# Rotated scores as two float32r products on stacked parts, and three steps moved in a hand-written order

## The chip, the cores and the metric

The kernel runs on one core of a Trainium2 chip. The metric is the device time of one execution in microseconds (us); the median over several runs is compared.

## The reference, cut to what matters

Two layers over `x` of 256 tokens by 1024 channels, all in float32. In each layer RMSNorm gives `h`, one combined projection of `h` feeds three branches, and each branch is multiplied by its own SiLU gate, projected back to 1024 channels, weighed by a sigmoid gate and summed. An output projection, another RMSNorm and the residual end the layer.

```python
# A: chunked gMLP.  sv is linear in the tokens; group g has its own 128 x 128 matrix
sv = einsum('gij,bnjgc->bnigc', ws_masked, layernorm(v)) + bs
a  = u * sv
# B: latent attention, 8 heads, 128 plain + 64 rotated channels, one rotated key for all heads
q = concat([q_nope, rope(q_rope)]);  k = concat([k_nope, rope(k_rope) for every head])
s = where(key_chunk <= query_chunk, q @ k.T / sqrt(192), -1e30)     # chunks of 64 tokens
b = softmax(s) @ v
# C: a causal convolution of width 4, then a gated linear recurrence over the tokens
xc = conv(x_c);  r, i = sigmoid(blocks(xc, w_a) + b_a), sigmoid(blocks(xc, w_x) + b_x)
```

The scores of one head are thus a product over 128 plain channels plus a product over 64 rotated ones.

## The kernel before, in words

**Precision.** A float32 product is slow on TensorE, and a float32r product is quicker but rounds its operands. Most products therefore work on operands in two parts: `hi` is the value rounded to float32r, `lo` the rest, and hi x hi + hi x lo + lo x hi is added up in PSUM (`mm3`; L307, L308, L309, or L431 to L433 where tokens are the rows of the result). The attention products are float32 products on whole values (L728 to L731, L770, L771).

**Weights.** They come in chunks, which are loaded, split and used in a fixed order: a DMA into a ring of three `raw` buffers, ScalarE's copy to `whi` (L268), VectorE's subtract to `wlo` (L269). There are three `whi`/`wlo` pairs. When a step has done with its chunk, it frees the pair, and the split of a later chunk is issued at that point on ScalarE and VectorE, behind what they already have in their queues. The table `LATE` says behind which stage of a step that is; for the query chunks (`uq`) it is stage 3, after the rotation, for `u` the end of its products.

**Order.** No scheduler orders the work. The table `ORDER` (L51 to L63) names the steps of a layer, and each step issues its instructions on all engines when its turn comes; every engine runs its own queue in that order. The steps that matter here:

- `uq` j: the queries of heads 2j and 2j + 1, rotated by VectorE (L645 to L647) into `qr`. Both heads share one tile: head 2j has partitions 0 to 63, head 2j + 1 partitions 64 to 127.
- `attend` i: the scores of heads 2i and 2i + 1 (i < 4), then `flip`, the transposes of the softmax of pair i - 1 (L759, six 128x128 blocks), then the `values` of pair i - 2 (L770, L771), then the softmax of pair i on VectorE and ScalarE (L737 to L752). So attend 4 has flip(3) and values(2), attend 5 has values(3).
- `split` g: the two parts `xh`, `xl` of the recurrence's input of group g: ScalarE's copy (L452) and VectorE's subtract (L453), of 128x1280 each.
- `norm` 0: the LayerNorm of `v` into `vn` (VectorE and GpSimd, L807 to L811). `stack` 0: copies of `xh` and `xl` into stacked tiles (VectorE's casts L449, ScalarE, GpSimd).
- `u` j, `za` j: two projections, then gMLP's gate. `za` j takes its projection into a bank, then the products with the gate matrix (L843, eight on 128 columns) into another one, `pm`; then ScalarE takes the sigmoid (L847) and VectorE multiplies (L848, L849) and reads `pm` (L852, twice).

**Rotated keys.** `krt[0]` has the rotated keys in partitions 0 to 63 and zeros in the others, `krt[1]` the other way round. The product of the shared `qr` tile with `krt[a]` so gives head 2i + a alone, at the price of half the rows being zero.

**PSUM.** There are two rings of banks: `bank`, five, for projections and scores, and `aux`, three (L133), for transposes, values, `pm` and others. A ring gives its banks out in turn, whoever asks; whoever gets one waits until its last user has been read.

Of the kernel before, what the change touches and what calls it, by code (L numbers as in the profile page):

```python
# [7 lines left out]
F32 = mybir.dt.float32  # L8
F32R = mybir.dt.float32r
AF = mybir.ActivationFunctionType  # L10
ALU = mybir.AluOpType
AX = mybir.AxisListType

P = 128
L = 2
D = 1024
S = 256
# [10 lines left out]
H, HN, HR, HV = 8, 128, 64, 128  # L28
# [23 lines left out]
    ("wl", 0), ("xc", 0), ("turn", 0), ("xc", 1), ("conv", 0), ("uq", 0), ("conv", 1), ("xc", 2), ("ukv", 0),  # L52
    ("conv", 2), ("ukv", 1), ("decay", 0), ("ws", 0), ("xc", 3), ("uq", 1), ("attend", 0), ("shift", 0),
    ("uq", 2), ("v", 0),
    ("attend", 1), ("xc", 4), ("conv", 3), ("v", 1), ("conv", 4), ("uq", 3), ("attend", 2), ("split", 1),
    ("v", 2), ("v", 3), ("attend", 3), ("split", 0), ("norm", 0), ("u", 0), ("stack", 0), ("attend", 4),
# [38 lines left out]
def tile_trunk(ctx: ExitStack, tc, I, out):  # L95
    nc = tc.nc
    const = ctx.enter_context(tc.tile_pool(name="const", bufs=1))
# [8 lines left out]
    def nm(s):  # L106
        n_[0] += 1
        return f"{s}_{n_[0]}"

    def slot(s, shape, dt=F32):  # L110
        n = 1
        for v in shape:
            n *= v
        t = sp.tile([P, SLOT_W], dt, tag="slot", name=nm(s))
        v = t[:, :n]
        if len(shape) == 2:
            v = v.rearrange("p (a b) -> p a b", b=shape[1])
        return v
# [23 lines left out]
    def f(x):  # L142
        return x.bitcast(F32)

    def v2(x, b):
        return x.rearrange("p (a b) -> p a b", b=b)

    mm = nc.tensor.matmul
    act = nc.scalar.activation
    V = nc.vector  # L150
    G = nc.gpsimd
# [16 lines left out]
    for l in range(L):  # L168
        for j in range(4):
            c0, n = ((C_CQ, QR), (C_CQ + QR, KVR + HR))[j // 2]  # L170
# [102 lines left out]
    def loads_to(i):  # L273
        while state["dma"] <= min(i, len(chunks) - 1):
            load(chunks[state["dma"]])
            state["dma"] += 1
# [16 lines left out]
    def get(*key):  # L293
        assert ids[key] < state["split"], key
        return chunks[ids[key]]

    def done(c, **how):
        pairs.append(c.pair)
        pump(**how)

    def fin(c, key, stage, **how):
        if LATE.get(key, 0) == stage:
            done(c, **how)


    def mm3(ps, lh, ll, rh, rl, start, stop):
        mm(ps, lh, rh, start=start, stop=False)  # L307
        mm(ps, lh, rl, start=False, stop=False)  # L308
        mm(ps, ll, rh, start=False, stop=stop)  # L309
# [6 lines left out]
    sinT = const.tile([P, S], F32, name="sinT")  # L316
    cosK = const.tile([P, NT, 64], F32, name="cosK")
    sinK = const.tile([P, NT, 64], F32, name="sinK")
    krt = [const.tile([P, S], F32, name=f"krt{i}") for i in range(2)]
    hT = [const.tile([P, NT, KT, P], F32R, name=f"hT{i}") for i in range(2)]  # L320
    X = const.tile([P, NT, D], F32, name="X")
    xm = const.tile([P, 2, S], F32R, name="xm")
# [133 lines left out]
    with tc.manual_schedule():  # L456
# [7 lines left out]
        load(chunks[0], parts=2, mid=lambda: nc.sync.dma_start(X[:, 1], I["x"][0, P : 2 * P, :]))  # L464
        state["dma"] = 1
        loads_to(2)
        for i in range(2):
            G.memset(krt[i], 0.0)
        nc.sync.dma_start(cosT, I["cosT"])
        nc.sync.dma_start(sinT, I["sinT"])  # L470
        nc.sync.dma_start(cosK, I["cosK"].rearrange("(t p) f -> p t f", p=P))
# [59 lines left out]
        for l in range(L):  # L531
# [53 lines left out]
            for i in range(8):  # L585
                j, t = (i // NT, i % NT) if l == 0 else (i % 4, i // 4)
# [7 lines left out]
            def turn_ranks(_):  # L594
                for b in range(3):
                    ps2 = aux()
                    for i in range(2):
                        k = 2 * b + i
                        for t in range(NT):
                            o = ps2[:, i * S + t * P : i * S + (t + 1) * P]  # L600
                            if k < 5:
                                nc.tensor.transpose(o, cn[t][:, k * P : (k + 1) * P], ident)
                            else:
                                nc.tensor.transpose(o[:64], krr[t], ident)
                    for i in range(2):
                        k = 2 * b + i
                        o = ps2[:, i * S : (i + 1) * S]
                        if k < 5:
                            act(cT[0][:, k], o, AF.Copy, scale=pt[:, k : k + 1])
                            V.scalar_tensor_tensor(  # L610
                                cT[1][:, k], o, pt[:, k : k + 1], f(cT[0][:, k]), ALU.mult, ALU.subtract
                            )
                        else:
                            act(krt[0][:64], o[:64], AF.Copy)
                            act(krt[1][64:], o[:64], AF.Copy)


            q = [slot("q", (4, S)) for _ in range(2)]
            kk = [slot("k", (4, S)) for _ in range(2)]
            vv = [slot("vv", (D,)) for _ in range(NT)]  # L620
            qr = slot("qr", (4, S))
            xp = [slot("xp", (GT, S + 3)) for _ in range(2)]
            xc = [slot("xc", (GT, S)) for _ in range(2)]
            for g in range(2):
# [2 lines left out]
            def queries(j):  # L627
                c = get(l, "uq", j)
                ps, ps2 = bank(), bank()
                for i in range(2):  # L630
                    for k in range(3):
                        a = i * P
                        mm3(ps[:, i * S : (i + 1) * S], c.h(k, a, a + P), c.l(k, a, a + P),
                            cT[0][:, k], cT[1][:, k], k == 0, k == 2)
                for k in range(3):
                    mm3(ps2[:, :S], c.h(k, S, S + P), c.l(k, S, S + P), cT[0][:, k], cT[1][:, k], k == 0, k == 2)
                fin(c, "uq", 0)
                act(q[j // 2][:, (j % 2) * 2 : (j % 2) * 2 + 2], v2(ps, S), AF.Copy)
                fin(c, "uq", 1)
                qs, qa = tmp(), tmp()  # L640
                for a in range(4):
                    b = a ^ 1
                    act(qs[a * 32 : a * 32 + 32, :S], ps2[b * 32 : b * 32 + 32, :S], AF.Copy)
                fin(c, "uq", 2)
                V.tensor_tensor(qa[:, :S], ps2[:, :S], cosT, ALU.mult)  # L645
                V.tensor_tensor(qs[:, :S], qs[:, :S], sinT, ALU.mult)
                V.tensor_tensor(qr[:, j], qa[:, :S], qs[:, :S], ALU.add)  # L647
                fin(c, "uq", 3)

            def keys_values(j):  # L650
                c = get(l, "ukv", j)
                for i in range(2):
                    ps = bank()
                    for m in range(2):
                        a = (2 * i + m) * 256
                        for k in range(2):
                            mm3(ps[:, m * S : (m + 1) * S], c.h(k, a, a + P), c.l(k, a, a + P),
                                cT[0][:, 3 + k], cT[1][:, 3 + k], k == 0, k == 1)
                    act(kk[j][:, 2 * i : 2 * i + 2], v2(ps, S), AF.Copy)
                for t in range(NT):  # L660
                    ps = bank()
                    ts = slice(t * P, (t + 1) * P)
                    for k in range(2):
                        rh = c.hi[:, k].rearrange("p (h r) -> p h r", r=256)[:, :, P:]
                        rl = c.lo[:, k].rearrange("p (h r) -> p h r", r=256)[:, :, P:]
                        lh, ll = cT[0][:, 3 + k, ts], cT[1][:, 3 + k, ts]
                        mm(v2(ps, P), lh, rh, start=k == 0, stop=False)
                        mm(v2(ps, P), lh, rl, start=False, stop=False)
                        mm(v2(ps, P), ll, rh, start=False, stop=k == 1)
                    if t == 1:  # L670
                        fin(c, "ukv", 0)
                    act(vv[t][:, j * 512 : (j + 1) * 512], ps, AF.Copy)
                fin(c, "ukv", 1)
# [48 lines left out]
            def scores(i):  # L722
                scs = [bank(), bank()]
                for a, sc in enumerate(scs):
                    h = 2 * i + a
                    qn, kn, kr = q[h // 4][:, h % 4], kk[h // 4][:, h % 4], krt[a]
                    qp = qr[:, i]
                    mm(sc[:, 0:P], qn[:, 0:P], kn[:, 0:P], start=True, stop=False)  # L728
                    mm(sc[:, 0:P], qp[:, 0:P], kr[:, 0:P], start=False, stop=True)
                    mm(sc[:, P : 3 * P], qn[:, P:], kn, start=True, stop=False)  # L730
                    mm(sc[:, P : 3 * P], qp[:, P:], kr, start=False, stop=True)  # L731
                return scs

            def softmax(scs):
# [324 lines left out]
            r = rsqrt_sum(ss)  # L1059
# [53 lines left out]
```

## Time and profile before

| | us |
|---|---|
| median of 3 runs | 798.22 (797.47 to 798.29) |
| the profiled execution | 798.34 |
| its span, first to last instruction | 796.6 |
| mean granted TensorE clock | 0.997 |
| TensorE products busy | 788.1 (99%) |
| VectorE / ScalarE / GpSimd busy | 548.9 (69%) / 469.3 (59%) / 70.5 (9%) |
| queue of the weight loads, share of 16 DMA engines | 54.3% |

In the timeline's rows stand: start in us, duration in us (of all instructions of the row), engine, source line, operation, result and operands, shapes, number of instructions, and in brackets how long the engine was idle before it and what ended that. Products overlap, so a PE row's duration is longer than its step to the next. A float32 product shows as two instructions, a float32r product as one. 1.74 us of the profiled execution lie outside its span.

### The profile page before, as it was taken

What the parts mean: (1) busy time and instruction counts of PE and PEld (TensorE: products, weight loads), DVE (VectorE), ACT (ScalarE), POOL (GpSimd) and SP (SyncE); (2) the same over time, 40 slices, a digit from 0 to 9 for tenths busy, and PEclk for the clock granted to TensorE, in tenths of its full rate; (3) what the DMA queues carried; (4) which work ended last, traced back from release to release, by engine and by line L of the source; (5) the groups of instructions that cost most, each with busy time, mean ns of one, the idle gap of its engine ahead of it and who ended that gap; (6) DMA issues with size and microseconds to landing.
All of it is one profiled execution on the core that took longest, in us unless ns stands there. A gap on an engine that the chain in (4) does not pass through costs nothing.

```text
span 796.6 us, 15355 instructions
## 1 busy us (share of the span) xinstructions
PE 788.1 (99%) x6445; PEld 780.2 (98%) x6445; DVE 548.9 (69%) x712; ACT 469.3 (59%) x689; POOL 70.5 (9%) x110
## 2 busy tenths in 40 slices
PE   9999999999999999999999999999999999999996
PEld 8999999999999999999999999999999999999996
DVE  5587788666876787555666868776578578775562
ACT  5785767339855736343567776654595584544441
POOL 1100503003000000000010032031210000000000
PEclk9999999999999999999999999999999999999998
DMA  7845454344666565666357626541575656564531
GB/s 229 290 152 182 153 161 155 112 122 137 201 213 211 159 215 169 199 212 216 109 171 239 208 94 211 159 128 51 166 219 167 221 162 202 185 214 150 193 132 54
DMA packets 134205, 137.87 MB, mean 173 GB/s; under 512 B 11046, under 2 KB 130808, under 8 KB 134136
## 3 DMA queue, kind: packets, MB, share of 16 engines
q1 hardware_dynamic: 134120, 136.90, 54.3%
q8 instruction: 50, 0.82, 0.4%
q14 instruction: 19, 0.16, 0.1%
q10 hardware_dynamic: 16, 0.00, 0.0%
HBM read 135.83 MB, written 1.05 MB: 172 GB/s over the span
## 4 chain that ended last, share of the span: by engine, by line
PE 94%; DMA 2%; issue 1%; DVE 1%; ACT 1%; SPq 0%; POOL 0%; POOLq 0%; DVEq 0%; ACTq 0%
PE mm L308 25%; PE mm L307 25%; PE mm L309 25%; PE mm L431 2%; PE mm L433 2%; PE mm L432 2%; DMA raw<-in_w_in_dram 1%; PE aux L843 1%; PE mm L730 1%; PE aux L770 1%; PE mm L731 1%; DMA X<-in_x_dram 1%; PE mm L549 1%; PE aux L1021 1%; PE mm L1020 1%
## 5 line engine op out<-in xcount | busy, mean ns | idle before, releaser
L269 DVE TENSOR_TENSOR wlo<-raw,whi 128x2048 fp32r<-128x2048 f32 (+5 forms) x123 | 264.6, 2156 | 115.9 <-ACT whi L268 115.5
L307 PE MATMUL mm<-hT,whi 128*128 128x256 f32 x1088 | 307.1, 282 | 0.0
L309 PE MATMUL mm<-hT,wlo 128*128 128x256 f32 x1088 | 305.8, 281 | 0.3 <-DVE wlo L269 0.3
L308 PE MATMUL mm<-hT,whi 128*128 128x256 f32 x1088 | 305.6, 281 | 0.0
L268 ACT ACTIVATE whi<-raw 128x2048 fp32r<-128x2048 f32 (+5 forms) x123 | 221.0, 1802 | 66.6 <-PE mm L308 26.8
L309 PEld LDWEIGHTS mm<-hT,wlo 128*128 128x128 f32 x1088 | 205.0, 188 | 0.5 <-DVE wlo L269 0.5
L307 PEld LDWEIGHTS mm<-hT,whi 128*128 128x128 f32 x1088 | 205.0, 188 | 0.0
L308 PEld LDWEIGHTS mm<-hT,whi 128*128 128x128 f32 x1088 | 205.0, 188 | 0.0
L973 ACT ACTIVATE t<-mm 128x512 f32<-128x512 f32 x18 | 10.8, 598 | 52.2 <-PE mm L309 52.2
L397 POOL TENSOR_TENSOR rstd<-rstd,mhalf 128x1 f32<-128x1 f32 x8 | 4.4, 551 | 391.1 <-DVE rstd L396 391.1
L308 PE MATMUL mm<-yc,whi 128*128 128x256 f32 x128 | 36.0, 282 | 0.0
L308 PE MATMUL mm<-ya,whi 128*128 128x256 f32 x128 | 36.0, 282 | 0.0
L307 PE MATMUL mm<-ya,whi 128*128 128x256 f32 x128 | 36.0, 281 | 0.0
L307 PE MATMUL mm<-yc,whi 128*128 128x256 f32 x128 | 36.0, 281 | 0.0
L431 PE MATMUL mm<-whi,hT 128*128 128x256 f32 x128 | 36.0, 281 | 0.0
L308 PE MATMUL mm<-yb,whi 128*128 128x256 f32 x128 | 35.9, 281 | 0.0
L309 PE MATMUL mm<-ya,wlo 128*128 128x256 f32 x128 | 35.9, 280 | 0.0
L309 PE MATMUL mm<-yc,wlo 128*128 128x256 f32 x128 | 35.9, 280 | 0.0
L309 PE MATMUL mm<-yb,wlo 128*128 128x256 f32 x128 | 35.8, 280 | 0.0
L307 PE MATMUL mm<-yb,whi 128*128 128x256 f32 x128 | 35.8, 280 | 0.0
L432 PE MATMUL mm<-wlo,hT 128*128 128x256 f32 x128 | 35.8, 279 | 0.0
L433 PE MATMUL mm<-whi,hT 128*128 128x256 f32 x128 | 35.7, 279 | 0.0
(279 smaller groups left out, 1663.4 us busy)
## 6 DMA issues: line engine op xcount, KB each, us to landing
raw<-in_w_in_dram SPq DMA_DIRECT2D x76, 1024.0 KB
raw<-in_w_proj_a_dram SPq DMA_DIRECT2D x8, 1024.0 KB
raw<-in_w_proj_b_dram SPq DMA_DIRECT2D x8, 1024.0 KB
raw<-in_w_proj_c_dram SPq DMA_DIRECT2D x8, 1024.0 KB
raw<-in_w_out_dram SPq DMA_DIRECT2D x8, 1024.0 KB
raw<-in_mla_w_uq_dram SPq DMA_DIRECT2D x8, 576.0 KB
raw<-in_mla_w_ukv_dram SPq DMA_DIRECT2D x4, 1024.0 KB
raw<-in_w_in_dram SPq DMA_DIRECT2D x4, 640.0 KB
```

The lines of the kernel that those rows point to most:

```text
L268: act(hi[:, w], c.raw[:, w], AF.Copy)
L269: V.tensor_tensor(lo[:, w], c.raw[:, w], f(hi[:, w]), ALU.subtract)
L307: mm(ps, lh, rh, start=start, stop=False)
L308: mm(ps, lh, rl, start=False, stop=False)
L309: mm(ps, ll, rh, start=False, stop=stop)
L431: mm(ps, lh, rh, start=k == 0, stop=False)
L432: mm(ps, lh, rl, start=False, stop=False)
L433: mm(ps, ll, rh, start=False, stop=k == KT - 1)
L549: mm(ps, ll, rh, start=False, stop=j % 2 * 4 + k == KT - 1)
L730: mm(sc[:, P : 3 * P], qn[:, P:], kn, start=True, stop=False)
L731: mm(sc[:, P : 3 * P], qp[:, P:], kr, start=False, stop=True)
L973: act(sg, ps, AF.Sigmoid)
```

## The change

**Scores.** `qr` now has a tile of its own per head, in float32r. The 64 rows of the head's own half hold the rounded part of its rotated query, the 64 rows of the other half the rest. `krt[0]` holds the rounded part of the rotated key in both halves, `krt[1]` the rest of it in both halves. The product of `qr` with `krt[0]` then adds hi x hi and lo x hi in one pass over 128 rows, the one with `krt[1]` hi x lo and lo x lo. Each head has two float32r products of 128 columns and two of 256 in place of one float32 product of each. The plain part stays float32. `krt` is no longer cleared by GpSimd. `queries` issues two copies (ScalarE) and two subtracts (VectorE) of 64x256 a chunk, after `fin(c, "uq", 3)`, so behind the split of the next weight chunk; the rotated keys get two subtracts a layer. The two tiles take one more of the 16 large slots.

**Order.** ("split", 1) moves from behind ("attend", 2) to behind ("u", 0). ("attend", 4) moves from before ("za", 0) to behind it.

```diff
--- before.py
+++ after.py
@@ -52,9 +52,9 @@
     ("wl", 0), ("xc", 0), ("turn", 0), ("xc", 1), ("conv", 0), ("uq", 0), ("conv", 1), ("xc", 2), ("ukv", 0),
     ("conv", 2), ("ukv", 1), ("decay", 0), ("ws", 0), ("xc", 3), ("uq", 1), ("attend", 0), ("shift", 0),
     ("uq", 2), ("v", 0),
-    ("attend", 1), ("xc", 4), ("conv", 3), ("v", 1), ("conv", 4), ("uq", 3), ("attend", 2), ("split", 1),
-    ("v", 2), ("v", 3), ("attend", 3), ("split", 0), ("norm", 0), ("u", 0), ("stack", 0), ("attend", 4),
-    ("za", 0), ("u", 1), ("za", 1), ("attend", 5), ("u", 2), ("za", 2), ("u", 3), ("za", 3), ("ga", 0),
+    ("attend", 1), ("xc", 4), ("conv", 3), ("v", 1), ("conv", 4), ("uq", 3), ("attend", 2),
+    ("v", 2), ("v", 3), ("attend", 3), ("split", 0), ("norm", 0), ("u", 0), ("split", 1), ("stack", 0), ("za", 0),
+    ("attend", 4), ("u", 1), ("za", 1), ("attend", 5), ("u", 2), ("za", 2), ("u", 3), ("za", 3), ("ga", 0),
     ("la", 0), ("lx", 0), ("r1", 0), ("stack", 1), ("pa", 0), ("ga", 1), ("pa", 1), ("la", 1), ("r2", 0),
     ("r3", 0), ("ga", 2), ("pa", 2), ("zb", 0), ("ga", 3), ("zb", 1), ("lx", 1), ("gb", 0), ("zb", 2),
     ("zb", 3), ("r1", 1), ("pa", 3), ("pb", 0), ("r2", 1), ("gb", 1), ("pb", 1), ("r3", 1), ("zc", 0),
@@ -316,7 +316,7 @@
     sinT = const.tile([P, S], F32, name="sinT")
     cosK = const.tile([P, NT, 64], F32, name="cosK")
     sinK = const.tile([P, NT, 64], F32, name="sinK")
-    krt = [const.tile([P, S], F32, name=f"krt{i}") for i in range(2)]
+    krt = [const.tile([P, S], F32R, name=f"krt{i}") for i in range(2)]
     hT = [const.tile([P, NT, KT, P], F32R, name=f"hT{i}") for i in range(2)]
     X = const.tile([P, NT, D], F32, name="X")
     xm = const.tile([P, 2, S], F32R, name="xm")
@@ -464,8 +464,6 @@
         load(chunks[0], parts=2, mid=lambda: nc.sync.dma_start(X[:, 1], I["x"][0, P : 2 * P, :]))
         state["dma"] = 1
         loads_to(2)
-        for i in range(2):
-            G.memset(krt[i], 0.0)
         nc.sync.dma_start(cosT, I["cosT"])
         nc.sync.dma_start(sinT, I["sinT"])
         nc.sync.dma_start(cosK, I["cosK"].rearrange("(t p) f -> p t f", p=P))
@@ -611,14 +609,16 @@
                                 cT[1][:, k], o, pt[:, k : k + 1], f(cT[0][:, k]), ALU.mult, ALU.subtract
                             )
                         else:
-                            act(krt[0][:64], o[:64], AF.Copy)
-                            act(krt[1][64:], o[:64], AF.Copy)
+
+                            for r in (slice(0, HR), slice(HR, P)):
+                                act(krt[0][r], o[:HR], AF.Copy)
+                                V.tensor_tensor(krt[1][r], o[:HR], f(krt[0][:HR]), ALU.subtract)
 
 
             q = [slot("q", (4, S)) for _ in range(2)]
             kk = [slot("k", (4, S)) for _ in range(2)]
             vv = [slot("vv", (D,)) for _ in range(NT)]
-            qr = slot("qr", (4, S))
+            qr = [slot("qr", (4, S), F32R) for _ in range(2)]
             xp = [slot("xp", (GT, S + 3)) for _ in range(2)]
             xc = [slot("xc", (GT, S)) for _ in range(2)]
             for g in range(2):
@@ -644,8 +644,15 @@
                 fin(c, "uq", 2)
                 V.tensor_tensor(qa[:, :S], ps2[:, :S], cosT, ALU.mult)
                 V.tensor_tensor(qs[:, :S], qs[:, :S], sinT, ALU.mult)
-                V.tensor_tensor(qr[:, j], qa[:, :S], qs[:, :S], ALU.add)
+                V.tensor_tensor(qa[:, :S], qa[:, :S], qs[:, :S], ALU.add)
                 fin(c, "uq", 3)
+
+
+                for a in range(2):
+                    own, other = (slice(i * HR, (i + 1) * HR) for i in (a, 1 - a))
+                    to = qr[j // 2][:, j % 2 * 2 + a]
+                    act(to[own], qa[own, :S], AF.Copy)
+                    V.tensor_tensor(to[other], qa[own, :S], f(to[own]), ALU.subtract)
 
             def keys_values(j):
                 c = get(l, "ukv", j)
@@ -723,12 +730,11 @@
                 scs = [bank(), bank()]
                 for a, sc in enumerate(scs):
                     h = 2 * i + a
-                    qn, kn, kr = q[h // 4][:, h % 4], kk[h // 4][:, h % 4], krt[a]
-                    qp = qr[:, i]
-                    mm(sc[:, 0:P], qn[:, 0:P], kn[:, 0:P], start=True, stop=False)
-                    mm(sc[:, 0:P], qp[:, 0:P], kr[:, 0:P], start=False, stop=True)
-                    mm(sc[:, P : 3 * P], qn[:, P:], kn, start=True, stop=False)
-                    mm(sc[:, P : 3 * P], qp[:, P:], kr, start=False, stop=True)
+                    qn, kn, qp = q[h // 4][:, h % 4], kk[h // 4][:, h % 4], qr[h // 4][:, h % 4]
+                    for o, ts, n in ((sc[:, 0:P], slice(0, P), P), (sc[:, P : 3 * P], slice(P, S), S)):
+                        mm(o, qn[:, ts], kn[:, :n], start=True, stop=False)
+                        mm(o, qp[:, ts], krt[0][:, :n], start=False, stop=False)
+                        mm(o, qp[:, ts], krt[1][:, :n], start=False, stop=True)
                 return scs
 
             def softmax(scs):
```

TensorE around attend 4 in the first layer, before (L759 transposes, L770 and L771 values; `aux_86` to `aux_88` are the three banks of the ring; the products of u 0 stand ahead of these rows, those of za 0 and then L843 into `aux_88` behind them):

```order
L759 MATMUL aux_88<-ident,t_75 128x128 [waits DVE_49,Activation_49]
L759 MATMUL aux_88<-ident,t_75 128x128 [waits DVE_49]
L759 MATMUL aux_88<-ident,t_75 128x128
L759 MATMUL aux_86<-ident,t_76 128x128 [waits DVE_49,Activation_49]
L759 MATMUL aux_86<-ident,t_76 128x128 [waits DVE_49]
L759 MATMUL aux_86<-ident,t_76 128x128
L770 MATMUL aux_87<-t_73,vv_387 128x256 [waits Activation_49]
L771 MATMUL aux_87<-t_73,vv_388 128x128
L770 MATMUL aux_87<-t_74,vv_387 128x256
L771 MATMUL aux_87<-t_74,vv_388 128x128
```

and with the change, where L849 is the gate product of za 0, L765 the transposes, L776 and L777 the values:

```order
L849 MATMUL aux_88<-wst_790,vn_979 128x128 [waits DVE_49,Activation_49]
L849 MATMUL aux_88<-wst_790,vn_980 128x128 [waits DVE_49]
L849 MATMUL aux_88<-wst_790,vn_979 128x128
L849 MATMUL aux_88<-wst_790,vn_980 128x128
L765 MATMUL aux_86<-ident,t_75 128x128 [waits Activation_49]
L765 MATMUL aux_86<-ident,t_75 128x128 x2
L765 MATMUL aux_87<-ident,t_76 128x128 [waits Activation_49]
L765 MATMUL aux_87<-ident,t_76 128x128 x2
L776 MATMUL aux_88<-t_73,vv_385 128x256 [waits DVE_49]
L777 MATMUL aux_88<-t_73,vv_386 128x128
L776 MATMUL aux_88<-t_74,vv_385 128x256
L777 MATMUL aux_88<-t_74,vv_386 128x128
```

The transposes and the values now stand behind za 0's gate products. The ring gives `aux_88` to the gate products, `aux_86` and `aux_87` to the transposes, and `aux_88` again to the values, which wait for a semaphore of VectorE (`DVE_49`) where they waited for one of ScalarE (`Activation_49`). In the second layer it is the same with `aux_87`.

VectorE in the same place, from the second tile of the LayerNorm to the reading of za 0's gate products, before:

```order
L811 TENSOR_SCALAR vn_963<-vn_963,st_32_399 128x1024
L269 TENSOR_TENSOR wlo_95<-raw_90,whi_94 128x2048
L449 CAST xs_1469<-xh_1406 64x512 x2
L449 CAST xm<-xl_1407 64x512 x2
L848 TENSOR_TENSOR t_79<-mm_81,t_79 128x512
L849 TENSOR_TENSOR t_79<-mm_85,t_79 128x512
L852 SCALAR_TENSOR_TENSOR t_80<-aux_88,pt_349,shift_404 128x256 x2
```

and with the change (L817, L854, L855 and L858 are the former L811, L848, L849 and L852):

```order
L817 TENSOR_SCALAR vn_980<-vn_980,st_33_398 128x1024
L269 TENSOR_TENSOR wlo_95<-raw_90,whi_94 128x2048
L453 TENSOR_TENSOR xl_1499<-xc_392,xh_1498 128x1280
L449 CAST xs_1502<-xh_1435 64x512 x2
L449 CAST xm<-xl_1436 64x512 x2
L854 TENSOR_TENSOR t_77<-mm_81,t_77 128x512
L855 TENSOR_TENSOR t_77<-mm_85,t_77 128x512
L858 SCALAR_TENSOR_TENSOR t_78<-aux_88,pt_347,shift_403 128x256 x2
```

The `xl` of split 1 has moved in between the weight split `wlo` and the casts of stack 0; before it stood some 30 rows earlier, behind the softmax of pair 2.

## The prediction

> **What bounds the kernel now.** I read the page's shares and the chain of waits first, then what TensorE (PE) waits for over the whole run.
>
> ```profile
> PE 788.1 (99%) x6445; PEld 780.2 (98%) x6445; DVE 548.9 (69%) x712; ACT 469.3 (59%) x689; POOL 70.5 (9%) x110
> PE 94%; DMA 2%; issue 1%; DVE 1%; ACT 1%; SPq 0%; POOL 0%; POOLq 0%; DVEq 0%; ACTq 0%
> ...
> PE aux L479 <- POOL ones L457: 1.0, 1, 1.0
> PE mm L549 <- DVE hT L505: 0.5, 1, 0.5
> PE mm L309 <- DVE wlo L269: 0.3, 1, 0.3
> ```
>
> The first row is busy time by engine, the second the chain that ended last by engine, the other three are all the waits of PE there are (us in total, times, longest). PE is busy in 788.1 of 796.6 us and waits 1.8 us in all. So two things pay in full: any time taken from a PE product, and any new wait of PE. VectorE (DVE) and ScalarE (ACT) have idle time, but only between the waits that tie them to PE.
>
> **The change: the products.** One head's scores before the change, on PE (start, us, instructions):
>
> ```profile
> 70.52 0.28 PE L307 MATMUL mm<-cT,whi 128*128 128x256 f32 x1
> 70.64 0.28 PE L308 MATMUL mm<-cT,whi 128*128 128x256 f32 x1
> 70.88 0.38 PE L728 MATMUL mm<-k,q 128*128 128x128 f32 x2
> 71.10 0.39 PE L729 MATMUL mm<-krt,qr 128*128 128x128 f32 x2
> 71.32 0.60 PE L730 MATMUL mm<-k,q 128*128 128x256 f32 x2
> 71.75 0.59 PE L731 MATMUL mm<-krt,qr 128*128 128x256 f32 x2
> 72.19 0.38 PE L728 MATMUL mm<-k,q 128*128 128x128 f32 x2
> ```
>
> Durations overlap, so the cost is the step from start to start. A float32 product is two instructions: L729 holds PE for 71.32 - 71.10 = 0.22 us, L731 for 72.19 - 71.75 = 0.44 us. A float32r product of 256 columns (L307, L308, operands in two parts) is one instruction with a step of 0.12 us. Two of them in place of L731 cost 0.24: a gain of 0.20 us a head. A float32r product of 128 columns is nowhere in this trace. If only the columns counted, it would step at half of 0.12, and two would cost 0.12 against 0.22 (a gain of 0.10). If it ran as slowly as the float32 product of its size, two would cost 0.44 (a loss of 0.22). The nearest row with one instruction on 128 columns and a fresh weight tile each is the transpose L759, shown below: six in 127.70 - 127.04 = 0.66 us, 0.11 each. I take 0.11, so that two cost what one float32 product did, and this half gains nothing. A head thus gains 0.20 (0.30 and -0.02 at the ends), a step of attention, two heads, 0.40 (0.60 and -0.04), and 16 heads 3.2 us (4.8 and -0.3).
>
> **The splits.** Each of eight query chunks adds two ACT copies and two DVE subtracts of 64x256, and each layer two DVE subtracts for the rotated keys. Nearest rows: 0.38 us a copy, 0.43 a DVE operation.
>
> ```profile
> L614 ACT ACTIVATE krt<-aux x2: 378/378/378, 41.9 to 431.6; 64x256 f32<-64x256 f32 x2
> ...
> 44.61 2.29 DVE L269 TENSOR_TENSOR wlo<-raw,whi 128x2048 fp32r<-128x2048 f32 x1 [2.77 <-ACT whi L268]
> 75.22 2.29 DVE L269 TENSOR_TENSOR wlo<-raw,whi 128x2048 fp32r<-128x2048 f32 x1 [0.72 <-ACT whi L268]
> 112.43 0.18 DVE L749 RECIPROCAL sum<-sum 128x4 f32<-128x4 f32 x1 [1.65 <-ACT t L747]
> ```
>
> That is 0.76 us of ACT and 0.86 of DVE a chunk. The brackets give DVE's idle time: behind the keys 2.77 us, behind the query chunks 0.72 and 1.65 us. PE hardly waits for DVE today, so I cost the splits at nothing. Without that cover they would be 0.9 us a chunk, 7 us in all. The two memsets that leave POOL save nothing, with POOL at 9%. No DMA is added or moved.
>
> **The moved steps.** Here the sum is decided. What PE does at the place in question, first layer:
>
> ```profile
> 127.04 0.82 PE L759 MATMUL aux<-ident,t 128*128 128x128 f32 x6
> 127.70 0.60 PE L770 MATMUL aux<-t,vv 128*128 128x256 f32 x2
> ...
> 128.93 0.36 PE L307 MATMUL mm<-hT,whi 128*128 128x256 f32 x1
> ...
> 134.69 1.05 PE L843 MATMUL aux<-wst,vn 128*128 128x128 f32 x8
> 135.50 0.36 PE L307 MATMUL mm<-hT,whi 128*128 128x256 f32 x1
> ```
>
> Six transposes (L759) and attention's values (L770, L771) take 128.93 - 127.04 = 1.89 us. Then comes za 0's projection, then its gate products L843, and at 135.50 projection u 1 starts. After the change the 1.89 us stand behind L843. All three kinds take banks of the `aux` ring, which has three: L843 one, the transposes two, and the values get the one that L843 has just filled. They must wait until DVE's L852 has read it. Before the change they took a bank that ACT had emptied long ago. DVE up to that L852:
>
> ```profile
> 126.70 1.49 DVE L453 TENSOR_TENSOR xl<-xc,xh 128x1280 fp32r<-128x1280 f32 x1
> ...
> 130.61 0.87 DVE L811 TENSOR_SCALAR vn<-vn,st 128x1024 f32<-128x1024 f32 x1 [0.45 <-POOL st L810]
> 131.40 2.48 DVE L269 TENSOR_TENSOR wlo<-raw,whi 128x2048 fp32r<-128x2048 f32 x1
> 133.80 1.16 DVE L449 CAST xs<-xh 64x512 fp32r<-64x512 f32 x2
> 134.98 1.06 DVE L449 CAST xm<-xl 64x512 fp32r<-64x512 f32 x2
> 136.06 0.69 DVE L848 TENSOR_TENSOR t<-mm,t 128x512 f32<-128x512 f32 x1
> 136.79 0.69 DVE L849 TENSOR_TENSOR t<-mm,t 128x512 f32<-128x512 f32 x1
> 137.40 0.86 DVE L852 SCALAR_TENSOR_TENSOR t<-aux,pt,shift 128x256 f32<-128x256 f32 x2
> ```
>
> From 131.40 on DVE has no gap: L852 ends at 138.26 because of the queue ahead of it. The second moved step puts one more `xl` (1.49 us, as at 126.70) into that queue, between `wlo` and the casts. What ties this stretch of DVE to PE lies earlier:
>
> ```profile
> 116.66 0.29 PE L433 MATMUL mm<-whi,hT 128*128 128x256 f32 x1
> 117.03 1.91 ACT L268 ACTIVATE whi<-raw 128x2048 fp32r<-128x2048 f32 x1 [1.12 <-issue]
> 118.98 2.29 DVE L269 TENSOR_TENSOR wlo<-raw,whi 128x2048 fp32r<-128x2048 f32 x1 [0.62 <-ACT whi L268]
> ```
>
> The last product of v 3 ends at 116.95, ACT's copy into the freed buffer starts at 117.03, DVE's subtract follows the copy. By then three of the layer's four steps of scores have run, so this anchor, and L852 with it, moves ahead by 3 x 0.40 = 1.20 us. L852 ends at 138.26 - 1.20 + 1.49 = 138.55. PE, four steps of scores ahead, has ended L843 at 135.50 - 1.60 - 1.89 = 132.01 and its six transposes at 132.67. It then **waits 5.9 us** for DVE. Queued behind the values are u 1 and everything after. The values take 128.93 - 127.70 = 1.23 us, and u 1 starts at 139.78 in place of 135.50: **4.28 us late**, the products' gain already taken off. The second layer is the same to a few hundredths:
>
> ```profile
> 524.76 0.36 PE L307 MATMUL mm<-hT,whi 128*128 128x256 f32 x1
> ...
> 526.65 0.87 DVE L852 SCALAR_TENSOR_TENSOR t<-aux,pt,shift 128x256 f32<-128x256 f32 x2
> ```
>
> 527.52 - 1.20 + 1.49 + 1.23 = 529.04 against 524.76, again 4.28. Together 8.6 us; at the ends of the products' gain (0.60 and -0.04 a step) the anchor moves by 1.80 or by -0.12, so 7.4 or 11.2 us. PE has no other idle time out of which the loss could be made up.
>
> **The clock.** A PE that stands still is throttled in this trace. At the start and the end of the run:
>
> ```profile
> 0.99 6.33 PE L479 MATMUL aux<-ones 128*128 128x128 f32 x28 [0.99 <-POOL ones L457]
> 7.26 0.22 PE L514 MATMUL aux<-ident,t 8*128 8x8 f32 x1
> ...
> 789.70 0.28 PE L1021 MATMUL aux<-whs,mg 128*128 128x256 f32 x1
> ...
> 790.00:792.00 2.00, 0.00 (x0) 0.00 (x0) 1.07 (x3) 0.47 (x2) 0.55 (x1) 1.00 0.00 0
> 792.00:794.00 2.00, 0.00 (x0) 0.00 (x0) 0.96 (x3) 0.00 (x0) 0.00 (x0) 0.56 0.49 176
> 794.00:797.00 3.00, 0.00 (x0) 0.00 (x0) 0.00 (x0) 0.00 (x0) 0.00 (x0) 0.50 0.18 60
> ```
>
> PE's last product ends at 789.98. In the three windows the granted clock (the last figure but two) is 1.00, 0.56 and 0.50: it halves at about 792.2, 2.3 us after PE stopped. A stall of 5.9 us is longer than that. At the start 28 instructions of L729's shape take 7.26 - 0.99 = 6.27 us, 0.224 each where the step is 0.11 at full speed: PE ran at half speed for 6.3 us of steady work, and lost 3.1. So a stall costs between nothing more (the clock holds) and 3.1 us more. I take 2.5, near the start's figure, a little below it because the start is a single case from a cold chip. Two stalls: 5.0 us.
>
> The Trainium skill's page "TensorE: Matmul & The Clock Gate" (Part 1: The HAM clock gate) says that the clock falls to half after an idle window of about 3.4 us, and comes back after one busy window of the same length. By its figure half speed would cost an estimated 1.7 us a stall and the sum would be some 1.6 us lower; the trace's 2.3 us to the fall and 6.3 us of slow start show that a single window isn't all that counts, so the rows are used.
>
> **The sum.** 798.34 (the profiled execution; the median of the runs, 798.22, lies 0.12 below) + 8.6 + 5.0 = 811.9, or **811.8 us** as a median.
>
> **The rivals.** (1) The stall comes, but the clock holds, or falls so late that little is lost. For it: only the end of the run shows the fall, and nothing there says that a stall between products counts alike. Against: 5.9 is well over 2.3 us. 798.3 + 8.6 = 806.9. (2) The float32r product of 128 columns is as slow as a float32 one, so nothing is gained: 798.3 + 11.2 + 5.0 = 814.5. For it: no row of such a product exists. Against: the transposes' 0.11. (3) The values find their bank free, PE doesn't stall, and the products' gain remains: 798.3 - 3.2 = 795.1, faster (793.5 with 4.8). The place is the second L852 of za 0, which would have to end by PE's 132.67 rather than 138.55; it decides from there on. Against: between 130.61 and L852's end DVE has 0.87 + 2.48 + 1.16 + 1.06 + 0.69 + 0.69 + 0.86 = 7.8 us of work without the moved `xl`, and `vn` itself waits for POOL. For it: only that DVE loses an `xl` some 13 us earlier, which the anchor at 117.03 doesn't pass on. (4) The stall is half as long, because DVE's queue runs 2.9 us further ahead than the anchor says: 798.3 + 8.6 - 5.8 = 801.1, and up to 804 with some loss of clock.
>
> **How the numbers follow.** Forecast 0.58, rival 1 0.20, rival 2 0.10, rival 3 0.07, rival 4 0.05. The time is the forecast's; its own range is 808.5 to 814. The range for 8 in 10 runs from rival 1 with the larger gain (798.2 + 7.4 = 805.6) to rival 2 with a little more (816). A measurement of this kernel can tell about 0.2%, 1.6 us, from no change: rivals 1, 2, 4 and the forecast all lie above it, rival 3 below. I leave 0.03 of rival 3 to the case in which a little is lost elsewhere and it ends within. Faster 0.06, same 0.03, slower 0.91.
>
> **What would show it.** Right, if PE's waits have a new row, the values' product on `aux` waiting for DVE's L858 (the changed file's number for L852), twice, near 5.9 us, and if the granted clock is under 1.00 in the windows right behind them. Steps of 0.12 for the two 256-column float32r products and 0.11 for the 128-column ones would confirm the gain; 0.06 or 0.22 its ends. The sum is wrong if that row is absent or under 2 us, if PE waits longer for `wlo` or a bank behind the query splits, or if za 0's L858 ends before PE's transposes do.

## The result

The changed kernel takes **819.56 us** (median) against 798.25 for the kernel before on the same chip, a ratio of 1.0255 (95% interval 1.0224 to 1.0286): slower. The prediction said slower, 811.8 us, with a range up to 816.0; the measured time lies 3.6 us above that range. One of the four executions took 1284.88 us at a mean granted clock of 0.557; the ratio leaves it out. The profiled execution took 819.68 us, its span is 817.7.

From the page of the changed kernel, busy time and the chain that ended last; then all that PE waits for (us in total, times, longest):

```profile
PE 792.7 (97%) x6445; PEld 784.4 (96%) x6445; DVE 558.1 (68%) x732; ACT 473.6 (58%) x705; POOL 71.4 (9%) x108
PE 90%; DVE 5%; issue 2%; ACT 1%; DMA 1%; POOL 1%; SPq 0%; POOLq 0%; DVEq 0%; ACTq 0%
...
PE aux L776 <- DVE t L858: 13.4, 2, 6.7
PE aux L849 <- DVE vn L817: 2.2, 4, 0.8
PE mm L545 <- ACT hT L501: 1.3, 1, 1.3
PE aux L477 <- POOL ones L457: 1.0, 1, 1.0
PE mm L547 <- DVE hT L503: 0.5, 1, 0.5
```

The first row of waits is the one forecast: the values' products wait for DVE to read za 0's gate products, once a layer. It is 6.7 us, not 5.9, and there is a second one ahead of it, L849 waiting for `vn`. PE is busy 4.6 us longer than before although its products got quicker, a sign of half speed. The place in the first layer, on PE, and the granted clock there (last figure but two of a window):

```profile
132.49 0.46 PE L849 MATMUL aux<-wst,vn 128*128 128x128 f32 x2 [0.34 <-DVE vn L817]
133.71 0.94 PE L849 MATMUL aux<-wst,vn 128*128 128x128 f32 x6 [0.76 <-DVE vn L817]
134.49 0.82 PE L765 MATMUL aux<-ident,t 128*128 128x128 f32 x6
142.00 1.22 PE L776 MATMUL aux<-t,vv 128*128 128x256 f32 x2 [6.69 <-DVE t L858]
143.01 0.64 PE L777 MATMUL aux<-t,vv 128*128 128x128 f32 x2
...
137.00:138.00 1.00, 0.00 (x0) 0.00 (x0) 1.00 (x2) 1.00 (x1) 0.96 (x2) 0.78 0.67 95
138.00:142.00 4.00, 0.00 (x1) 0.01 (x1) 3.86 (x9) 0.01 (x1) 0.93 (x2) 0.50 0.69 238
142.00:146.00 4.00, 4.00 (x14) 3.64 (x15) 3.47 (x3) 1.99 (x4) 0.00 (x0) 0.50 0.00 1
146.00:147.00 1.00, 1.00 (x6) 1.00 (x6) 0.00 (x0) 0.00 (x0) 0.00 (x0) 0.50 0.74 127
147.00:148.00 1.00, 1.00 (x7) 1.00 (x6) 0.00 (x0) 0.00 (x0) 0.00 (x0) 0.60 1.03 367
148.00:149.00 1.00, 1.00 (x11) 1.00 (x10) 0.00 (x0) 0.00 (x0) 0.00 (x0) 1.00 1.08 383
```

PE's last transpose ends at 135.31, the clock halves at about 137.6, 2.3 us later, and is full again at about 147.8. So PE works at half speed from 142.0 to 147.8. Half of that, 2.9 us, is an estimate of the loss; a run below, at full clock, gives 2.7.

Where the time went is seen by subtracting the start of the k-th product before from that of the k-th after (both have 6445; the stretches end where the two orders have the same product in that place). Positive is late:

| stretch of the program | us gained or lost |
|---|---|
| the start, up to the first layer's scores | +0.9 |
| first layer, four steps of scores | -1.7 |
| first layer, za 0 and attend 4 | +11.3 |
| from there to the second layer's scores | +0.5 |
| second layer, four steps of scores | -1.4 |
| second layer, za 0 and attend 4 | +11.2 |
| the rest | +0.4 |
| sum (span 817.7 - 796.6) | +21.1 |

The products gained 3.1 us (the rows are rounded). What was underestimated is the two places at attend 4: 11.2 us each, where the prediction had 5.9 of wait and 2.5 of clock, 8.4. Of the 11.2, 2.7 are clock and 8.5 waiting: 6.85 for L858 (142.00 less 135.15, where the last of six transposes with a step of 0.11 has had its turn), and the rest the two waits for `vn`. PE loses a little more by a wait than its bracket shows, because the bracket counts from the end of the product before, and products otherwise overlap.

One head's scores after the change:

```profile
71.81 0.38 PE L735 MATMUL mm<-k,q 128*128 128x128 f32 x2
71.94 0.30 PE L736 MATMUL mm<-krt,qr 128*128 128x128 f32 x1
72.08 0.28 PE L737 MATMUL mm<-krt,qr 128*128 128x128 f32 x1
72.20 0.65 PE L735 MATMUL mm<-k,q 128*128 128x256 f32 x2
72.49 0.47 PE L736 MATMUL mm<-krt,qr 128*128 128x256 f32 x1
72.80 0.28 PE L737 MATMUL mm<-krt,qr 128*128 128x256 f32 x1
72.92 0.38 PE L735 MATMUL mm<-k,q 128*128 128x128 f32 x2
```

From head to head it is 72.92 - 71.81 = 1.11 us, where it was 72.19 - 70.88 = 1.31: the 0.20 us forecast.

VectorE is where the forecast broke. Its rows in the same layer:

```profile
112.03 0.87 DVE L655 TENSOR_TENSOR qr<-t,qr 64x256 fp32r<-64x256 f32 x2
...
114.50 0.17 DVE L745 TENSOR_SCALAR max<-max 128x6 f32<-128x6 f32 x1
...
116.52 0.18 DVE L755 RECIPROCAL sum<-sum 128x4 f32<-128x4 f32 x1 [1.65 <-ACT t L753]
118.31 2.29 DVE L269 TENSOR_TENSOR wlo<-raw,whi 128x2048 fp32r<-128x2048 f32 x1 [0.50 <-ACT whi L268]
121.19 2.28 DVE L269 TENSOR_TENSOR wlo<-raw,whi 128x2048 fp32r<-128x2048 f32 x1
...
135.98 1.68 DVE L453 TENSOR_TENSOR xl<-xc,xh 128x1280 fp32r<-128x1280 f32 x1
...
141.07 0.87 DVE L858 SCALAR_TENSOR_TENSOR t<-aux,pt,shift 128x256 f32<-128x256 f32 x2
```

The reciprocal of pair 2's softmax stands at 116.52; before it stood at 112.43, so it is 4.1 us late, of which 0.9 comes from the start. Yet the idle time in its bracket is 1.65 us in both. That bracket, which the prediction had taken for room, is ScalarE's share of the same softmax: DVE's maximum, ScalarE's exponentials, DVE's sum. A split ahead of the maximum moves both ends of it, and the splits do stand there: L655 at 112.03, the maximum behind it. The `wlo` that the prediction tied to PE (118.98 before) is at 121.19 and has no idle time ahead of it any more.

### The profile page after: what moved, and what is told of

Its sections match the earlier page's. It is cut to its first block, busy times and chain, and to the rows that moved or that the text cites. A ratio compares the mean times of both kernels' runs of the same rounds, so it can differ in the third digit from the quotient of the medians.

```text
span 817.7 us, 15387 instructions
## 1 busy us (share of the span) xinstructions
PE 792.7 (97%) x6445; PEld 784.4 (96%) x6445; DVE 558.1 (68%) x732; ACT 473.6 (58%) x705; POOL 71.4 (9%) x108
## 4 chain that ended last, share of the span: by engine, by line
PE 90%; DVE 5%; issue 2%; ACT 1%; DMA 1%; POOL 1%; SPq 0%; POOLq 0%; DVEq 0%; ACTq 0%
PE mm L308 23%; PE mm L307 23%; PE mm L309 23%; PE mm L431 2%; PE mm L432 2%; PE mm L433 2%; DVE wlo L269 1%; PE mm L547 1%; PE mm L546 1%; PE mm L545 1%; PE mm L735 1%; PE aux L776 1%; DVE xl L453 1%; PE aux L1026 1%; PE aux L1025 1%
```

## The experiments

The theory after this comparison has three parts. The stall is made by the three-bank ring and the moves. It is longer than forecast because the splits, costed at nothing, delay VectorE. And the clock takes another 2.9 us (by the estimate above) behind each stall. The rivals: the stall has to do with the splits alone; the splits are hidden, and the moved `xl` is what made the stall longer; the clock costs nothing beside the wait.

**The products and splits alone.** The old order table in the changed kernel.

```diff
-    ("attend", 1), ("xc", 4), ("conv", 3), ("v", 1), ("conv", 4), ("uq", 3), ("attend", 2),
-    ("v", 2), ("v", 3), ("attend", 3), ("split", 0), ("norm", 0), ("u", 0), ("split", 1), ("stack", 0), ("za", 0),
-    ("attend", 4), ("u", 1), ("za", 1), ("attend", 5), ("u", 2), ("za", 2), ("u", 3), ("za", 3), ("ga", 0),
+    ("attend", 1), ("xc", 4), ("conv", 3), ("v", 1), ("conv", 4), ("uq", 3), ("attend", 2), ("split", 1),
+    ("v", 2), ("v", 3), ("attend", 3), ("split", 0), ("norm", 0), ("u", 0), ("stack", 0), ("attend", 4),
+    ("za", 0), ("u", 1), ("za", 1), ("attend", 5), ("u", 2), ("za", 2), ("u", 3), ("za", 3), ("ga", 0),
```

> The changed kernel with the old order table: the products and splits alone. Theory A (the splits weren't hidden: each delays the softmax behind it on VectorE, because the idle time there is ScalarE's part of the same softmax): with split 1 back in its old place softmax 3 ends some 1.4 us later than the 128.95 us it has in the changed kernel, about 130.4, while PE comes to the transposes of pair 3 at about 126.0. PE waits some 4 us there in each layer, the clock falls, about 2.9 us more are lost, and the run takes 806 to 812 us. Theory B (the splits are hidden, as the prediction had it): PE waits under 1 us, and the run takes 795 to 797 us.

Measured 806.23 us, a ratio of 1.0094 (1.0081 to 1.0108). Waits, and the place in the first layer:

```profile
PE aux L765 <- DVE t L757: 6.1, 2, 3.1
...
129.81 1.07 PE L765 MATMUL aux<-ident,t 128*128 128x128 f32 x6 [3.12 <-DVE t L757]
```

The transposes wait 3.1 us a layer for softmax 3, where they waited for nothing before. Its theory A holds, with a wait somewhat shorter than the 4 us expected. With these splits on VectorE the quicker products make this kernel slower under either order, here by 0.9%.

**The moves alone.** The kernel before with the new order table (the lines above with their signs exchanged).

> The kernel before with the new order table: the moves alone. If the moves and the three-bank ring make the stall: za 0's second L852 ends near 138.26 + 1.6 = 139.9, PE has ended the transposes at 134.3, waits 5.6 us, and loses 2.9 us more to the clock: 8.5 us a layer, 815 us (812 to 818). If the stall needs the splits: PE waits under 2 us, 797 to 801 us.

Measured 815.61 us, 1.021 (1.0196 to 1.0224).

```profile
PE aux L770 <- DVE t L852: 11.0, 2, 5.7
```

The stall needs no splits: order and ring make it, 5.7 us where the sum gave 5.6.

**The bank clash taken away.** The values of pair 2 are issued ahead of za 0, only the transposes of pair 3 behind it. Values and gate products then have different banks.

```diff
-    ("v", 2), ("v", 3), ("attend", 3), ("split", 0), ("norm", 0), ("u", 0), ("split", 1), ("stack", 0), ("za", 0),
+    ("v", 2), ("v", 3), ("attend", 3), ("split", 0), ("norm", 0), ("u", 0), ("split", 1), ("stack", 0), ("vals", 2), ("za", 0),
...
-                if 0 <= i - 2 < 4:
+                if 0 <= i - 2 < 4 and i != 4:
                     values(i - 2, hd["T", i - 2])
...
-                "attend": attend, "v": gate_values, "norm": gate_norm, "split": conv_split, "stack": conv_stack,
+                "attend": attend, "vals": lambda i: values(i, hd["T", i]), "v": gate_values, "norm": gate_norm, "split": conv_split, "stack": conv_stack,
```

> The changed kernel, but the values of pair 2 are issued ahead of za 0 and only the transposes of pair 3 behind it, so that the values and za 0's gate products have different banks. If the bank is the whole stall: PE doesn't wait for L858, the clock stays at 1.00, the wait for vn falls to about 0.2 us a layer because PE comes 1.2 us later, and 3.2 us of gain from the products remain, less about 1 us at the start: 796.5 us (795 to 799), at or under the kernel before. If PE only waits elsewhere instead (for wlo, or for the transposes' operands): 802 to 812 us.

Measured 797.11 us, 0.9987 (0.9978 to 0.9996). PE waits for nothing in attention or at the gate, and 22.4 us of the changed kernel's time are gone. Against the kernel before, the 0.13% that it is quicker hardly count; but the place of four products decides whether the change costs 21 us or nothing.

**The clock's share.** 22 products whose result isn't used stand between the transposes and the values of attend 4.

```diff
+                if i == 4:
+                    w = bank()
+                    for _ in range(22):
+                        mm(w[:, :P], ones, ones, start=True, stop=True)
                 if 0 <= i - 2 < 4:
                     values(i - 2, hd["T", i - 2])
```

> The changed kernel with 22 idle products of 128 columns (about 4.9 us, result not used) between the transposes and the values of attend 4, so that PE is busy while it would wait. If half speed behind the stall costs 2.9 us in each layer: the clock stays at 1.00 there and the run takes about 813.8 us (812.5 to 815.5). If the clock costs nothing beside the wait: 819.6 us or more.

Measured 813.41 us, 6.2 less than without them. The values start at the same time, but at full speed:

```profile
135.20 5.08 PE L789 MATMUL mm<-ones 128*128 128x128 f32 x44
142.05 0.70 PE L776 MATMUL aux<-t,vv 128*128 128x256 f32 x2 [1.78 <-DVE t L862]
...
138.00:142.00 4.00, 2.27 (x21) 2.08 (x19) 3.89 (x8) 0.07 (x1) 0.96 (x2) 1.00 0.70 242
142.00:146.00 4.00, 3.95 (x30) 3.85 (x31) 3.50 (x3) 1.88 (x4) 0.00 (x0) 1.00 0.02 1
```

142.05 against 142.00: the wait ends when it did, and the clock stays at 1.00. The medians differ by 3.1 us a layer. The two traces put it lower: the products from the values on take 2.7 us less in the first layer and 2.6 in the second.

**The splits' share.** The query splits' subtracts on GpSimd in place of VectorE, all else as changed; and the same with the old order.

```diff
-                    V.tensor_tensor(to[other], qa[own, :S], f(to[own]), ALU.subtract)
+                    G.tensor_tensor(to[other], qa[own, :S], f(to[own]), ALU.subtract)
```

> The changed kernel with the query splits' two subtracts a chunk on GpSimd in place of VectorE; order and ring as changed. If the prediction's sum failed because VectorE's splits put its queue behind PE: za 0's L858 ends some 2.5 us earlier, PE's wait for it falls from 6.7 to about 5 us and the wait for vn (1.1 us a layer) nearly goes, and the time falls to 813 to 815 us, near the prediction's 811.8. If the splits don't matter to the stall: 819 us.

> The same subtracts on GpSimd, with the old order table. If VectorE's splits caused the 3.1 us wait a layer before the transposes with the old order: it falls under 0.7 us and the products' gain shows: 796 us (795 to 798). If that wait has another cause (the products' earlier PE, ScalarE's copies): 803 to 806 us, as with the splits on VectorE (806.2).

With the new order 812.27 us (1.0171, 1.0151 to 1.0191), with the old one 797.74 (0.9987, 0.9978 to 0.9995). PE's waits in the first, and DVE's `wlo` behind v 3 in it:

```profile
PE aux L776 <- DVE t L858: 11.7, 2, 5.9
...
117.27 2.29 DVE L269 TENSOR_TENSOR wlo<-raw,whi 128x2048 fp32r<-128x2048 f32 x1 [0.22 <-ACT whi L268]
```

The stall is 5.9 us, where 5 was expected, the wait for `vn` is gone, and `wlo` stands at 117.27; the prediction had worked out 5.9 and 117.78. Against the splits on VectorE it is 7.3 us under the new order and 8.5 under the old. Not all of the 7.3 is the splits' doing: in the two traces 5.5 us of the difference lie at the two places (11.25 and 11.16 against 8.67 and 8.24), and 1.4 at the start, which is told below. So the splits' part of the theory holds: it is VectorE's 0.9 us a chunk, sixteen subtracts in all. On GpSimd a pair of them takes up to 3.4 us, but PE doesn't wait for it.

**The two moves apart.** There are two of them, split 1 and attend 4 (za 0 only comes earlier by them). Split 1 moved with attend 4 in its old place, and the other way round.

```diff
 # split 1 alone
-    ("v", 2), ("v", 3), ("attend", 3), ("split", 0), ("norm", 0), ("u", 0), ("split", 1), ("stack", 0), ("za", 0),
-    ("attend", 4), ("u", 1), ("za", 1), ("attend", 5), ("u", 2), ("za", 2), ("u", 3), ("za", 3), ("ga", 0),
+    ("v", 2), ("v", 3), ("attend", 3), ("split", 0), ("norm", 0), ("u", 0), ("split", 1), ("stack", 0), ("attend", 4),
+    ("za", 0), ("u", 1), ("za", 1), ("attend", 5), ("u", 2), ("za", 2), ("u", 3), ("za", 3), ("ga", 0),
 # attend 4 alone
-    ("attend", 1), ("xc", 4), ("conv", 3), ("v", 1), ("conv", 4), ("uq", 3), ("attend", 2),
-    ("v", 2), ("v", 3), ("attend", 3), ("split", 0), ("norm", 0), ("u", 0), ("split", 1), ("stack", 0), ("za", 0),
+    ("attend", 1), ("xc", 4), ("conv", 3), ("v", 1), ("conv", 4), ("uq", 3), ("attend", 2), ("split", 1),
+    ("v", 2), ("v", 3), ("attend", 3), ("split", 0), ("norm", 0), ("u", 0), ("stack", 0), ("za", 0),
```

> Products and splits as changed, split 1 moved, attend 4 in its old place. Taking 1.3 to 1.5 us of split 1 out from ahead of softmax 3 should cut the transposes' wait from 3.1 to about 1.7 us a layer; that is shorter than the 2.3 us after which the clock fell, so little is lost to half speed: 799.5 us (798.5 to 801.5). If split 1's place doesn't matter: 806 us.

> Products and splits as changed, attend 4 moved, split 1 in its old place. The moved xl leaves the queue ahead of za 0's L858 (1.7 us less) but stands ahead of softmax 3 again (1.4 us more), so the stall stays within 0.5 us: 819 us (817.5 to 820.5). If the moved xl was what made the stall longer than the wait for the ring alone: 815 to 816.5 us.

Split 1 alone: 803.16 us (1.0058, 1.0044 to 1.0072), 3.7 above what I expected. Attend 4 alone: 818.08 (1.0244, 1.0225 to 1.0263), as expected. The second shows that the moved `xl` is not what makes the stall longer: out of the queue ahead of L858 it is back ahead of softmax 3 and `vn`. The waits there are 5.2 us for L858 and 2.3 a layer for `vn`. The first has the waits that I expected, 1.9 us a layer:

```profile
127.84 1.07 PE L765 MATMUL aux<-ident,t 128*128 128x128 f32 x6 [1.95 <-DVE t L757]
518.43 1.25 PE L765 MATMUL aux<-ident,t 128*128 128x128 f32 x6 [1.86 <-DVE t L757]
...
123.22:126.63 3.41, 2.67 (x23) 2.47 (x21) 2.15 (x8) 1.19 (x7) 0.00 (x0) 1.00 1.08 359
126.63:130.05 3.42, 2.21 (x15) 1.96 (x15) 2.82 (x8) 3.42 (x6) 0.00 (x0) 1.00 0.37 118
...
515.75:519.17 3.42, 1.56 (x12) 1.21 (x12) 1.68 (x8) 3.14 (x10) 0.00 (x0) 1.00 0.81 263
519.17:522.58 3.41, 3.41 (x14) 3.03 (x14) 2.38 (x4) 3.38 (x4) 1.62 (x4) 0.50 0.00 0
522.58:525.99 3.41, 3.41 (x31) 3.41 (x31) 3.14 (x2) 3.29 (x9) 3.29 (x4) 1.00 0.03 7
```

In the first layer the clock stays at 1.00 and PE falls 2.3 us back. In the second, after a wait that is no longer, it falls to half when PE is already at work again, and PE falls 3.9 us back. That is 1.6 us of the 3.7 missed. The rest is partly a wait of 0.7 us for a `wlo`, and isn't followed further.

The windows show why two waits of one length differ. Every change of the clock that a trace of this case records lies a whole number of steps of 3.41 us from every other change in that trace: in the changed kernel at 4.45, 11.28, 14.69, 137.57, 147.81, 536.93 and 547.17 us. Where the steps begin differs from execution to execution. The windows above are cut at these steps. In the first layer the wait is spread over two of them, with 0.74 and 1.21 us of idle PE (length less the first figure); in the second all 1.86 us lie in one, and the clock is at half in the next.

**Both causes taken away, and the price of a narrow product.** The values ahead of za 0 together with the subtracts on GpSimd; and, in the kernel with the values ahead, the second product of 128 columns left out.

```diff
-                        mm(o, qp[:, ts], krt[0][:, :n], start=False, stop=False)
-                        mm(o, qp[:, ts], krt[1][:, :n], start=False, stop=True)
+                        mm(o, qp[:, ts], krt[0][:, :n], start=False, stop=n == P)
+                        if n != P:
+                            mm(o, qp[:, ts], krt[1][:, :n], start=False, stop=True)
```

> The values of pair 2 ahead of za 0 (no bank clash) and the query splits' subtracts on GpSimd: both causes of the loss taken away. The theory so far (ring and splits are all of it) expects no wait of PE in attention or in gMLP's gate, all 3.2 us of the products' gain, and 0.5 to 0.9 us less than with the values ahead alone (797.1): 796.3 us (795 to 797). If GpSimd's use slows VectorE by as much as it takes off: 797 us or more, no better than with the values ahead alone.

> The kernel with the values ahead, without the second 128-column float32r product of each head (the product with krt[1] for the first 128 tokens is left out of the computation), to price one such product by the step of a head, 1.11 us with it. If it holds PE 0.11 us as the transposes do: 1.00 us a head. If the columns alone count: 1.05 us. If it is as slow as the float32 product of its size: 0.89 us.

The first takes **795.16 us**, 0.9954 (0.994 to 0.9968): faster than both kernels, and 3.9 us faster than the kernel before on the same chip: about all that the products can give. PE's waits in it are those of the start. The second took 797.67 us in its one run; a head in it:

```profile
71.06 0.38 PE L735 MATMUL mm<-k,q 128*128 128x128 f32 x2
71.19 0.30 PE L736 MATMUL mm<-krt,qr 128*128 128x128 f32 x1
71.34 0.65 PE L735 MATMUL mm<-k,q 128*128 128x256 f32 x2
71.63 0.47 PE L736 MATMUL mm<-krt,qr 128*128 128x256 f32 x1
71.94 0.28 PE L738 MATMUL mm<-krt,qr 128*128 128x256 f32 x1
72.06 0.38 PE L735 MATMUL mm<-k,q 128*128 128x128 f32 x2
```

72.06 - 71.06 = 1.00 us against 1.11: a float32r product of 128 columns holds PE for 0.11 us, as long as a transpose of the same shape and nearly as long as a float32r product of 256. Two of them cost what one float32 product of 128 columns does.

## Why the prediction was right or wrong

- **The products: right.** 0.20 us a head and 3.2 in all were forecast, 0.20 and 3.1 measured; the choice of 0.11 us for the narrow product was the right one of three.
- **The bank clash as the mechanism: right.** The row of waits that was named came, twice, and it went when the banks were kept apart (797.11 us). Rival 3 (no stall) is out.
- **"So I cost the splits at nothing": wrong, and the step that failed.** The idle times named as their cover, 0.72 and 1.65 us behind the query chunks, were no room. The 1.65 is half a round trip of the softmax and came back unchanged 4.1 us later. DVE fell behind PE by the splits, so the anchor behind v 3 gave 120.25 us (121.19 less the 0.94 of the start) where the sum had 117.78. With L858 late by the same, the stall grew from 5.9 to 6.7 us, although `vn`, late too, added two waits ahead of it, 1.1 us of idle time a layer together. PE so lost 8.5 us by waiting at each place, and 6.1 with the subtracts on GpSimd. The price that the prediction gave for the case without cover, 7 us, came near to the 7.3 of that run, but partly by luck: 5.5 of them lie at the two places, not 0.9 at each of eight chunks. It stood in the text but in no rival and not in the range. With the subtracts off VectorE, the sum's 811.8 meets 812.27, and so do its parts: 8.7 and 8.2 us at the two places where it had 8.4.
- **The clock: right in size, partly by luck.** 2.5 us a stall were taken; 2.7 and 2.6 were lost, by comparison with the run with idle products. Rival 1 is out. But the working behind the 2.5 doesn't hold. That the fall came 2.3 us after PE's last product, as at the end of the run before, is a coincidence: with the subtracts on GpSimd it came 4.5 us after, and in the run with split 1 alone when PE was already at work again. And what the slow start showed, 6.3 us at half speed, doesn't speak against a single window: before the change, the window from 0.36 to 3.78 us has 0.6 us of idle PE, the next one none, and the clock is full behind that one. The Trainium skill's page "TensorE: Matmul & The Clock Gate" (Part 1: The HAM clock gate) says that the window is free-running; the traces agree, with their steps of 3.41 us that begin at another time in each execution. Its advice to avoid gaps of over about 3 us (Why this matters for your kernels) is too generous here: a gap of 1.9 us was enough once.
- **The start: not foreseen, and not the change's.** The changed kernel's profile is 0.9 us late there, because the clock rose early (at 4.45 us, before the change at 7.19), PE ran ahead, had to wait 1.3 us for `hT` and was throttled again:

```profile
0.99 5.03 PE L477 MATMUL aux<-ones 128*128 128x128 f32 x28 [0.99 <-POOL ones L457]
9.65 0.44 PE L545 MATMUL mm<-whi,hT 128*128 128x384 f32 x1 [1.27 <-ACT hT L501]
```

  Two other kernels with the same start (the subtracts on GpSimd with the new order, split 1 moved alone) took 6.33 us for these 28 instructions, as the kernel before did, and had no such wait. It varies from execution to execution.
- **The size of the miss.** 7.8 us lie between 811.8 and 819.6. By the profile, 5.2 of them are the waiting at the two places (2 x (8.5 - 5.9)), all but 0.4 of which the splits account for: with the subtracts on GpSimd it is 6.1 a place. The clock's 0.3, the start's 0.9 and about as much in small steps elsewhere are of the size of the spread between runs and aren't told apart further.

## What to carry to other kernels

An idle bracket ahead of an instruction is cover only if what ends it doesn't move along with the work to be hidden. Where A waits for B and B for A's own earlier result, added work on A moves all of it, so follow each releaser one step further back before an edit is costed at nothing. When steps change places in a hand-written order, write down which buffer of each ring every user gets in the new order and who has to have read it: here a ring of three turned a slack of some microseconds into a stall, and moving four products back by one step undid it.

## What the runs showed of the hardware

- PE was throttled after far shorter gaps than a whole stall. In the traces it went by how the idle time fell into windows of 3.41 us, one behind the other, that begin at another time in each execution. In all twelve traces, the clock fell behind each window at full speed in which PE was idle for 1.82 us or more, and behind none with 1.68 or less; of two between, it fell behind 1.72 and not behind 1.78. So a wait of 1.86 us in one window was followed by half speed, one of 1.95 us spread over two was not, and 1.27 and 0.54 us in one window at the start were (1.82 in all).
- The clock came back behind a window in which PE was busy nearly throughout (0.5 us idle at most; 0.6 was too much). Half speed cost from 1.6 to 2.7 us a stall in eleven stalls of six kernels, by the same products at full speed in another trace.
- At the start, the same 28 warming products took from 4.77 to 6.33 us in the twelve profiles. The four in which they took 5.3 us or less lost the gain again: PE then waited 1.3 to 1.4 us for `hT` and was throttled.
- Small subtracts of 64x256 mostly took 0.42 us on VectorE and from 0.73 to 2.5 us on GpSimd, and the kernel was still faster with them on GpSimd.
